# A decoder block with an expert layer: the V rows of token block 1 gathered a token per partition and summed on VectorE, where TensorE summed them before

## The chip, the cores and the metric
One Trainium2 chip, one NeuronCore. The metric is the device time of one execution in microseconds (us), as the median of several. The kernel before has 2984.19 us (three runs, 2970.84 to 2986.44).

The engines are named as in the profile: PE is TensorE's matmuls and PEld its weight loads, DVE is VectorE, ACT ScalarE, POOL GpSimd and SP the sync engine, which here only issues DMAs.

## The reference, cut to what matters
One layer on 1024 tokens of width 1024, all float32: an input projection, an mLSTM and a differential attention over four heads each, an output projection, and then the part that the change touches, a retrieval of single-neuron experts for each token (`peer`):

```
s = einsum('thpk,hpnk->thpn', q, sub_keys)        # 8 heads, two halves of 128 keys
sv, si = top_k(s, 16); cand = sv0 + sv1; fv, fpos = top_k(cand, 16)
eidx = the 16 experts of each head; g = softmax(fv)      # 8 x 16 = 128 experts per token
act = gelu(einsum('td,thkd->thk', xb, u_tab[eidx]))
out = einsum('thk,thkd->td', g * act, v_tab[eidx])       # the sum over V rows
```

The two tables `u_tab` and `v_tab` have 16384 rows of 1024 numbers (4 KB a row). So a block of 128 tokens needs 128 x 128 rows of each: 128 gathers of 128 rows (512 KB each) of U, and as many of V.

## The kernel before, in words
**Blocks and groups.** The 1024 tokens are eight blocks of 128. They go through the front part (projections, mLSTM, attention, output projection, keys, top-k) in three groups: blocks 0 and 1, blocks 2 to 4, blocks 5 to 7 (`GROUPS`, L36).

**Two ways for the experts.** Blocks 2 to 5 (`DENSE`, L37) gather nothing: in the last part of the kernel (`dense`, L1274) they are multiplied with all rows of the tables, 128 steps of 128 experts; a step has a score part (`s_mm`, L1330, matmul L1343), a gate part on VectorE (`s_gate`, L1346) and a value part (`v_step`, L1363, matmul L1375). Their gates are laid out as tables by `gates` (L1212): VectorE writes one-hot tiles `oh` (L1258 and L1259, two buffers), TensorE multiplies them (`ps_g`, L1243), ScalarE copies the result (L1245), and it goes to DRAM. Blocks 0, 1, 6 and 7 gather.

**A gathered block.** `g_u` (L1018) gathers, for expert number k of each token, a U row per partition, and VectorE multiplies it with the token's row and sums over it (L1028). When all 128 are done, `g_w` (L1033) makes the weights w = g * gelu(z). Then come 128 gathers of V rows (`g_v`, L1070), in one of two forms:
- the blocks in `ROWSUM` (L39; 6 and 7) gather as for U, one row per token, with the index tile `ei`, and VectorE adds each tile, times one column of w, to a sum in PSUM (`g_v_rows`, L1054, L1062 and L1064). `finish_rows` (L1154) ends the block.
- the others (0 and 1) transpose w and the indices on TensorE (L1044 to L1051), so that gather t brings the 128 experts of token t, one per partition. Each gather is used in four matmuls (a 128x32 weight, which is a column of w in a strip of zeros, `strips`, L994, and 256 columns, L1090), which the trace counts as eight: 1024 for a block. Two gathers are used together, so they come in bursts of 16. VectorE copies two columns of weights into a strip now and then (L1088). `finish` (L1171) ends the block.

**Buffers.** All gathered tiles, U and V, share six buffers (`GB`, L997, tag `gx`). A gather waits, on POOL's queue, for the buffer that the use of an earlier one gives back. The sum `ga` is one PSUM tile for all blocks (L1040).

**Order of the work.** The gathers are one generator (`gathers`, L1104) that runs behind the other work: each step of a projection calls `tick` (L306), which advances it by `RG` = 1.6 gathers (L70); the use of a gather is written `LAG` = 4 gathers later (L1110). V goes before U, two by two. When the front part has been written, what is left of it is written with `later(PU)` (L1500), and the dense part with `later(PD)` (L1507). A planner (a list scheduler with its own estimate of durations) then fixes one order for each engine and queue: of the work that it believes ready, the one written earliest goes first; `later` moves work back in this ranking, `PU` = 100000 places and `PD` = 300000; the gates of block 5, written in the dense part, are taken forward again by `LP` = 310000 (L1430). So the ranks are: front, gates of block 5, left-over gathers, dense. On the chip each engine runs its order strictly, and waits in it.

The part around the change, V of block 1, stands beside these pieces of the third group: the output projection (`front_out`, L803, two calls of `proj_R`, matmul L423), the query projection and the scores (`front_keys`, L859, four calls of `proj_T`, matmul L403, and L879), top-16 on VectorE (`key_tops`, L895), the routing of blocks 5, 6 and 7 (`route`, L937), the gate tables of blocks 3 to 5, and the first 14 score parts of the dense steps (`AHEAD`).

```
def g_v_rows(o, k):                                    # L1054
    vt = gat.tile([P, D], F32, tag="gx", name="gvr", bufs=GB)
    nc.gpsimd.indirect_dma_start(out=vt, out_offset=None, in_=pv,
                                 in_offset=bass.IndirectOffsetOnAxis(ap=o.ei[:, k:k + 1], axis=0))
    ...
            nc.vector.scalar_tensor_tensor(o.acc, vt, o.w[:, k:k + 1], o.acc, op0=OP.mult, op1=OP.add)
...
                mm = nc.tensor.matmul(o.acc[c * 32:(c + 1) * 32, q * QW:(q + 1) * QW],      # L1090
                                      st[:, q, 31 + 32 * i - r:63 + 32 * i - r],
                                      vt[:, c * QW:(c + 1) * QW], start=r == 0 and q % 2 == 0, stop=r == 31 and q % 2 == 1)
```

Of the kernel before, what the change touches and what calls it, by code (L numbers as in the profile page):

```python
# [35 lines left out]
GROUPS = [2, 3, 3]  # L36
DENSE = [2, 3, 4, 5]  # L37
MIXED = []
ROWSUM = [6, 7]  # L39
GSC = 2.0 ** 14  # L40
PG = 100000
PU = 100000
# [9 lines left out]
def kernel(ctx: ExitStack, tc: tile.TileContext, x, c_col, ada_w, ada_b, ada_bc, n1c,  # L52
# [980 lines left out]
    def g_w(o):  # L1033
# [6 lines left out]
        o.acc = psg.tile([P, D], F32, tag="ga", name="ga")  # L1040
        if o.tb in ROWSUM:
            o.w = w
# [11 lines left out]
# [6 lines that stand above are left out]
        def use():  # L1060
            if k == 0:
                nc.vector.tensor_scalar(o.acc, vt, o.w[:, 0:1], None, op0=OP.mult)  # L1062
            else:
                nc.vector.scalar_tensor_tensor(o.acc, vt, o.w[:, k:k + 1], o.acc, op0=OP.mult, op1=OP.add)  # L1064
            if k == P - 1:
                finish_rows(o.tb, o.acc)
                summing.remove(o)
        return use

    def g_v(o, m):  # L1070
        if o.tb in ROWSUM:
            return g_v_rows(o, m)
        r, q = divmod(m, 4)
        t = q * 32 + r
        vt = gat.tile([P, D], F32, tag="gx", name="gv", bufs=GB)
        got = nc.gpsimd.indirect_dma_start(out=vt, out_offset=None, in_=pv,  # L1076
                                           in_offset=bass.IndirectOffsetOnAxis(ap=o.eT[:, t:t + 1], axis=0))
        o.held.append((r, q, vt))

        def use():  # L1080
            if m % VB != VB - 1:
                return
            first = True
            for r, q, vt in o.held[:VB]:
                st = strips[(r // SR) % 2]
                i = r % SR
                if i == 0 and q == 0:
                    nc.vector.tensor_copy(st[:, :, 31:31 + 32 * SR:32], o.wT[:, :, r:r + SR])  # L1088
                for c in range(4):
# [3 lines that stand above are left out]
                    if first:  # L1093
                        tc.add_manual_dep(mm.ins, got.ins.name, together, reason="a batch's tokens stand side by side")
                        first = False
            del o.held[:VB]
            if m == P - 1:
                finish(o.tb, o.acc)
                summing.remove(o)
        return use  # L1100
# [468 lines left out]
```

## Time and profile before
| what | value |
|---|---|
| median of three runs | 2984.19 us (2970.84 to 2986.44) |
| the profiled execution, its own time | 2968.57 us |
| its span in the trace | 2966.8 us |
| mean granted TensorE clock in it | 0.962 of 2.4 GHz |
| busy: PE, PEld, DVE, ACT, POOL | 2783.8, 2079.3, 2382.0, 972.9, 1275.8 us |
| HBM traffic | 302 GB/s over the span |

A profile row gives busy time and counts; "idle before" is the time in which an engine stood still in front of such an instruction, with what released it. Matmuls overlap in the pipe, so the busy time of a group is the union of its matmuls and not count times mean. In a table of stretches the numbers in brackets count instructions, PEclk is the granted TensorE clock as a share of 2.4 GHz, and "DMA share" the mean busy share of the 16 DMA engines. An entry of VectorE with an accumulator output counts as two instructions.

### The profile page before, as it was taken

How to read it: one execution, taken by the hardware profiler on the slowest of the kernel's cores; microseconds unless marked ns; L12 is line 12 of the kernel's file. 1: busy time of each engine (PE TensorE's matmuls, PEld its weight loads, DVE VectorE, ACT ScalarE, POOL GpSimd, SP SyncE). 2: the span in 40 equal slices, each digit the busy share in tenths (PEclk: the TensorE clock that was granted, in tenths of full speed). 3: DMA queues.
4: the chain of work that ended last, by engine and by line, in shares of the span. 5: the costliest groups of instructions: out<-in, count | busy, mean ns of one | idle time of the engine just before them, and what ended most of it. 6: DMA issues, size and time to landing. Idle time of an engine off the chain costs nothing.

```text
span 2966.8 us, 40093 instructions
## 1 busy us (share of the span) xinstructions
PE 2783.8 (94%) x13686; PEld 2079.3 (70%) x13686; DVE 2382.0 (80%) x5489; ACT 972.9 (33%) x1701; POOL 1275.8 (43%) x1083
## 2 busy tenths in 40 slices
PE   6899999689999988999998999999999999999998
PEld 5547757466555765765666887877887778777776
DVE  5634999955998687457988998888988889888896
ACT  1432344312235355232454332322332323322332
POOL 0000277654555453334644555544544445444430
PEclk9989999689999998999998999999999999999999
DMA  8845699999999888998888999999999999899982
GB/s 281 254 135 182 201 359 343 328 341 336 328 343 314 311 289 305 322 340 286 306 299 302 325 326 335 318 323 345 325 333 323 325 332 337 327 318 316 319 318 78
DMA packets 395809, 899.48 MB, mean 303 GB/s; under 512 B 34754, under 2 KB 183234, under 8 KB 391508
## 3 DMA queue, kind: packets, MB, share of 16 engines
q0 software_dynamic: 147456, 536.94, 50.4%
q1 hardware_dynamic: 248148, 359.98, 35.9%
q8 instruction: 108, 1.77, 0.2%
q14 instruction: 97, 0.79, 0.1%
HBM read 846.45 MB, written 50.35 MB: 302 GB/s over the span
## 4 chain that ended last, share of the span: by engine, by line
PE 45%; DVE 22%; DMA 17%; issue 11%; POOL 3%; ACT 2%; SPq 0%; DVEq 0%; POOLq 0%; ACTq 0%
PE ps_pj L403 9%; PE ps_pj L423 8%; DMA Gt<-G_d 8%; PE ps_dA L1375 7%; PE ps_dS L1343 7%; DVE gu L1028 5%; DVE ga L1064 3%; PE ps_g L1243 3%; PE ga L1090 3%; DMA gu<-in_peer_u_dram,ei 2%; POOL gvr L1057 2%; DMA wmod<-in_ada_w_dram 2%; DVE dvs L1369 2%; DMA gv<-in_peer_v_dram,eT 2%; DVE dacc L1382 2%
## 5 line engine op out<-in xcount | busy, mean ns | idle before, releaser
L1024 POOL DMA_INDIRECT gu<-in_peer_u_dram,ei x512 | 652.1, 1274 | 969.1 <-DVE sv L912 349.5
L1375 PE MATMUL ps_dA<-dvs,W 128*128 128x512 f32 x2976 | 720.1, 397 | 44.4 <-DVE dvs L1369 21.1
L1343 PE MATMUL ps_dS<-dhT,us 128*128 128x512 f32 x3072 | 729.1, 391 | 1.2 <-POOL us L1336 1.2
L1375 PEld LDWEIGHTS ps_dA<-dvs,W 128*128 128x128 f32 x2976 | 566.8, 191 | 175.2 <-DVE dvs L1369 24.7
L1028 DVE SCALAR_TENSOR_TENSOR gu<-gu,h2r 128x1024 f32<-128x1024 f32 x512 | 619.8, 1220 | 73.2 <-DMA gu<-in_peer_u_dram,ei 65.8
L1343 PEld LDWEIGHTS ps_dS<-dhT,us 128*128 128x128 f32 x3072 | 575.5, 188 | 129.2 <-issue 7.4
L1057 POOL DMA_INDIRECT gvr<-in_peer_v_dram,ei x256 | 302.0, 1180 | 326.9 <-DVE ga L1064 191.7
L1076 POOL DMA_INDIRECT gv<-in_peer_v_dram,eT x256 | 273.3, 1068 | 269.7 <-PE ga L1090 151.6
L1064 DVE SCALAR_TENSOR_TENSOR ga<-gvr,w,ga 128x1024 f32<-128x1024 f32 x254 | 325.2, 1280 | 1.3
L1368 ACT ACTIVATE dvs<-dv 128x512 fp32r<-128x512 f32 x248 | 154.7, 626 | 321.6 <-PE ps_dA L1375 183.9
L403 PE MATMUL ps_pj<-hT,wr 128*128 128x384 f32 (+1 forms) x768 | 234.2, 460 | 2.8 <-ACT ae L598 2.8
L403 PE MATMUL ps_pj<-h2T,wr 128*128 128x384 f32 (+1 forms) x768 | 231.2, 454 | 0.0
L1344 ACT ACTIVATE ge<-ps_dS 128x512 f32<-128x512 f32 x128 | 76.3, 597 | 455.2 <-PE ps_dS L1343 455.2
L1245 ACT ACTIVATE stg<-ps_g 128x512 f32<-128x512 f32 x128 | 133.7, 1062 | 232.4 <-PE ps_g L1243 188.4
L403 PEld LDWEIGHTS ps_pj<-hT,wr 128*128 128x128 f32 x768 | 145.3, 194 | 79.4 <-issue 9.4
L403 PEld LDWEIGHTS ps_pj<-h2T,wr 128*128 128x128 f32 x768 | 142.2, 190 | 73.3 <-issue 9.9
L1258 DVE TENSOR_TENSOR oh<-iotah,dT 128x1024 f16<-128x1024 f16 x128 | 94.8, 746 | 118.1 <-PE ps_g L1243 115.2
L1352 DVE SCALAR_TENSOR_TENSOR ge<-ge,Gt 128x512 f32<-128x512 f32 x128 | 90.9, 719 | 121.8 <-DMA Gt<-G_d 120.1
L423 PE MATMUL ps_pj<-wr,hT 128*128 128x256 f32 (+1 forms) x672 | 181.8, 424 | 3.0 <-DMA wr<-in_w_in_dram 2.1
L1369 DVE TENSOR_TENSOR dvs<-dv,dvs 128x512 fp32r<-128x512 f32 x248 | 167.6, 682 | 9.7 <-ACT dvs L1368 9.7
L1090 PE MATMUL ga<-gv,strip 128*32 128x256 f32 x2048 | 147.8, 398 | 14.1 <-DMA gv<-in_peer_v_dram,eT 14.1
L423 PEld LDWEIGHTS ps_pj<-wr,hT 128*128 128x128 f32 x672 | 129.0, 197 | 44.1 <-issue 22.5
(294 smaller groups left out, 3311.6 us busy)
## 6 DMA issues: line engine op xcount, KB each, us to landing
u<-in_peer_uT_dram SPq DMA_DIRECT2D x128, 512.0 KB
dv<-in_peer_v_dram SPq DMA_DIRECT2D x248, 256.0 KB
wr<-in_w_in_dram SPq DMA_DIRECT2D x168, 256.0 KB
G_d<-stg SPq DMA_DIRECT2D x32, 1024.0 KB
Gt<-G_d SPq DMA_DIRECT2D x15, 2048.0 KB
wmod<-in_ada_w_dram SPq DMA_DIRECT2D x48, 512.0 KB
wr<-in_peer_w_query_dram SPq DMA_DIRECT2D x96, 256.0 KB
wr<-in_w_out_dram SPq DMA_DIRECT2D x48, 256.0 KB
```

What stands on the lines that cost most here:

```text
L403: nc.tensor.matmul(out[f], w2[:, kh, f * P:(f + 1) * P], hT[:, kb, :n], start=kb == 0 and f % k == 0, stop=kb == NC - 1 and f % k == k - 1)
L423: nc.tensor.matmul(out[f], hT[:, kb, f * P:(f + 1) * P], wk[:, kh], start=kb == 0 and f % k == 0, stop=kb == NC - 1 and (f % k == k - 1 or ...
L1024: nc.gpsimd.indirect_dma_start(out=u, out_offset=None, in_=pu, in_offset=bass.IndirectOffsetOnAxis(ap=o.ei[:, k:k + 1], axis=0))
L1028: nc.vector.scalar_tensor_tensor(u, u, 1.0, o.h2, op0=OP.mult, op1=OP.mult, accum_out=o.z[:, k:k + 1])
L1057: nc.gpsimd.indirect_dma_start(out=vt, out_offset=None, in_=pv, in_offset=bass.IndirectOffsetOnAxis(ap=o.ei[:, k:k + 1], axis=0))
L1064: nc.vector.scalar_tensor_tensor(o.acc, vt, o.w[:, k:k + 1], o.acc, op0=OP.mult, op1=OP.add)
L1076: got = nc.gpsimd.indirect_dma_start(out=vt, out_offset=None, in_=pv, in_offset=bass.IndirectOffsetOnAxis(ap=o.eT[:, t:t + 1], axis=0))
L1090: mm = nc.tensor.matmul(o.acc[c * 32:(c + 1) * 32, q * QW:(q + 1) * QW], st[:, q, 31 + 32 * i - r:63 + 32 * i - r], vt[:, c * QW:(c + 1) * ...
L1343: nc.tensor.matmul(ps, us[:, a, c], hT[:, b, c, sl], start=c == 0 and i == 0, stop=c == NC - 1 and i == 2)
L1368: nc.scalar.activation(vs[:, 0], v, AF.Copy)
L1369: nc.vector.tensor_sub(vs[:, 1], v, vs[:, 0])
L1375: nc.tensor.matmul(pacc[tb], w[:, a, tb * P:(tb + 1) * P], vs[:, b], start=jj == 0 and i == 0, stop=jj == J - 1 and i == 2)
```

## The change
Block 1 joins the blocks whose V rows are gathered a token per partition and added on VectorE. Block 0 alone keeps the matmul form. Nothing else is edited; `g_w`, `g_v` and the planner's order follow from the list.

```diff
 GROUPS = [2, 3, 3]
 DENSE = [2, 3, 4, 5]
 MIXED = []
-ROWSUM = [6, 7]
+ROWSUM = [1, 6, 7]
 GSC = 2.0 ** 14
```

## Rows read from the trace of the kernel before
**Rows 1.** The page's head: span, then busy time of each engine.
```profile
span 2966.8 us, 40093 instructions
...
PE 2783.8 (94%) x13686; PEld 2079.3 (70%) x13686; DVE 2382.0 (80%) x5489; ACT 972.9 (33%) x1701; POOL 1275.8 (43%) x1083
```
**Rows 2.** Stretches: length, busy PE, PEld, DVE, ACT, POOL, then PEclk, DMA share, GB/s.
```profile
1190.00:1300.00 110.00, 106.83 (x725) 76.26 (x724) 40.76 (x97) 30.90 (x51) 40.31 (x40) 0.98 0.96 348
1300.00:1412.00 112.00, 110.47 (x732) 67.25 (x731) 83.33 (x445) 30.46 (x42) 47.76 (x45) 1.00 0.84 295
1412.00:1490.00 78.00, 72.28 (x501) 48.40 (x502) 76.41 (x283) 37.26 (x38) 47.91 (x36) 0.98 0.84 297
1490.00:1594.00 104.00, 93.72 (x649) 71.02 (x642) 86.00 (x132) 59.41 (x74) 50.27 (x35) 0.94 0.84 296
1594.00:2890.00 1296.00, 1262.70 (x5470) 1035.89 (x5470) 1161.38 (x1592) 386.84 (x583) 623.92 (x504) 0.99 0.93 327
2890.00:2967.00 77.00, 66.75 (x288) 53.20 (x286) 52.28 (x88) 18.16 (x41) 0.00 (x0) 0.97 0.23 79
```
**Rows 3.** The same stretches, tile `gv` alone: PE, PEld, POOL (block 1's V).
```profile
1190.00:1300.00 110.00, 20.09 (x274) 7.64 (x274) 40.31 (x40) 0.98 0.96 348
1300.00:1412.00 112.00, 22.68 (x334) 9.16 (x334) 43.05 (x43) 1.00 0.84 295
1412.00:1490.00 78.00, 18.04 (x237) 6.85 (x240) 30.60 (x29) 0.98 0.84 297
1490.00:1594.00 104.00, 13.71 (x186) 5.00 (x179) 19.80 (x18) 0.94 0.84 296
```
**Rows 4.** Groups by line: whole span (three rows), then VectorE from 1190 to 1412.
```profile
L1028 DVE SCALAR_TENSOR_TENSOR gu<-gu,h2r 128x1024 f32<-128x1024 f32 x512 | 619.8, 1220 | 73.2 <-DMA gu<-in_peer_u_dram,ei 65.8
L1064 DVE SCALAR_TENSOR_TENSOR ga<-gvr,w,ga 128x1024 f32<-128x1024 f32 x254 | 325.2, 1280 | 1.3
L1090 PE MATMUL ga<-gv,strip 128*32 128x256 f32 x2048 | 147.8, 398 | 14.1 <-DMA gv<-in_peer_v_dram,eT 14.1
...
L1088 DVE COPY strip<-wT 128x8 f32<-128x8 f32 x11 | 2.1, 200 | 9.0 <-PE ga L1090 9.0
```
**Rows 5.** Who waited for whom, 1190 to 1412: us in total, times, longest.
```profile
POOL gv L1076 <- PE ga L1090: 116.8, 34, 14.2
...
DVE oh L1258 <- PE ps_g L1243: 74.8, 19, 8.5
POOL gv L1076 <- DVE eT L1049: 26.8, 1, 26.8
```
**Rows 6.** The chain that ended last, 1337 to 1353: start us, us, what.
```profile
1337.07 6.45 PE ps_pj L403 x20
1343.52 1.00 PE ga L1090 x16
...
1351.18 1.49 PE ps_pj L403 x4
```
**Rows 7.** Groups by line: VectorE from 1412 to 1594, POOL from 1190 to 1594.
```profile
L1028 DVE SCALAR_TENSOR_TENSOR gu<-gu,h2r 128x1024 f32<-128x1024 f32 x4 | 7.1, 1766 | 0.0
...
L1336 POOL TENSOR_TENSOR us<-u,us 128x1024 fp32r<-128x1024 f32 x18 | 44.1, 2452 | 24.4 <-ACT us L1335 24.2
```
**Rows 8.** Stretches, columns as in rows 2: U of block 0 and 1; mid of dense.
```profile
400.00:500.00 100.00, 95.79 (x384) 64.87 (x384) 95.69 (x226) 43.59 (x100) 74.63 (x52) 0.93 0.96 338
500.00:600.00 100.00, 67.36 (x295) 47.44 (x293) 87.65 (x220) 36.45 (x101) 61.26 (x51) 0.73 0.92 327
...
2200.00:2300.00 100.00, 97.77 (x425) 80.41 (x424) 90.49 (x124) 29.16 (x45) 49.86 (x43) 0.98 0.94 331
```
**Rows 9.** Tile `gu` in a stretch: DVE, POOL; then VectorE's last V sum and `finish_rows`.
```profile
1700.00:1800.00 100.00, 44.96 (x76) 52.00 (x40) 1.00 0.96 336
...
2879.76 1.28 DVE L1064 SCALAR_TENSOR_TENSOR ga<-gvr,w,ga 128x1024 f32<-128x1024 f32 x1
...
2893.71 1.28 DVE L1168 SCALAR_TENSOR_TENSOR fx<-fx,gms 128x1024 f32<-128x1024 f32 x1
```

## The prediction
> **What bounds the kernel now.** I read the page's head first: TensorE is busy 94% of the span and VectorE 80% [rows 1], so the tempting reading is that work taken from TensorE is time gained. That is an average over stages. So next the stretches around block 1's V sums [rows 2], and in the same stretches the V tile alone [rows 3]. The tile's 128 gathers (40, 43, 29, then 18 less a few of neighbours at the cuts) run from 1190 us into the last of these four stretches: this is where the change acts. Four stages lie there. A, 1190 to 1300, the output projection: TensorE 106.8 of 110 us, VectorE only 40.8, DMA 0.96. B, 1300 to 1412, query projection and top-16: TensorE 110.5 of 112, VectorE 83.3. C, 1412 to 1490, the routing: VectorE 76.4 of 78, which is its limit. D, 1490 to 1594, block 5's gates ahead of the dense part: VectorE 86.0 and TensorE 93.7 of 104. After that the dense part: TensorE 1262.7 of 1296, VectorE 1161.4 (90%) [rows 2].
>
> Then the waits tell what VectorE's free time is [rows 5]. In A and B it stands 74.8 us before a one-hot tile until TensorE has read the older one: it waits because it is early, not because it has nothing to do, so this time is real room. POOL waits 116.8 us for TensorE to give gather buffers back, so the gathers are paced by their users and not by DMA. The dense part can't begin before routing and gates, and 14 score parts ahead are all that TensorE may do meanwhile; so the path to the dense part runs over TensorE in A and B and over VectorE from C on.
>
> **What the change removes.** (1) 1024 matmuls on TensorE, 74.5 us by the four stretches (20.1, 22.7, 18.0, 13.7) [rows 3], half of the 147.8 us of both blocks [rows 4]. (2) The disturbance of each burst: 20 projection matmuls in a row take 6.45 us, 0.32 each, but four behind a burst take 1.49 instead of 1.29 [rows 6]: 0.2 us for each of 64 bursts, 13 us. So TensorE loses some 87 us, of which A and B hold (20.1 + 22.7) x 87 / 74.5 = 50. (3) Sixteen strip copies of 0.2 us [rows 4], 3 us of VectorE, and the index transposes, for which POOL stood 26.8 us before the first V gather [rows 5]; the new gathers use the index tile that U used. (4) The block's end is four passes of 1024 columns on VectorE in either form; I count zero, and what hides a difference is that nothing waits for this block's output; without that cover it would be an operation or two, under 3 us.
>
> **What it adds.** 128 sums on VectorE at 1280 ns [rows 4], 164 us. The gathers stay 128 of the same 512 KB, on POOL and DMA alike, so both are costed at nothing.
>
> What could make a sum dearer is POOL's subtraction of 2452 ns (18 of them in C and D): beside it the U product takes 1766 ns instead of 1220 [rows 7, 4]. The bounds are 1.28 and 1.28 x 1766 / 1220 = 1.85 us for the sums that fall there, up to 51, so 0 to 29 us more; I take 1.28, since the row of the operation itself is nearest. The Trainium skill, SBUF — State Buffer, section Who interferes with whom, says that only a VectorE instruction with two inputs in SBUF contends with a GpSimd instruction that reads it. The sum has its second input in PSUM, so by that page the price is the lower bound, and no row before shows a sum beside a subtraction.
>
> **Where the 128 sums come to stand.** The projections of A and B have 16 and 32 ticks at 1.6 gathers, so 77 gathers are ranked among this front work; the other 51 rank behind the front and block 5's gates, but ahead of the dense part.
>
> *A to C.* VectorE has 200.5 us of work in these 300 us [rows 2]. The 77 sums add 98.6, the copies take off 3: 296 of 300. TensorE's 50 us would let the stage end earlier only if VectorE could follow, and it can't: it has become the limit here. The question is how densely it runs. The best long stretch of this trace in which it carries gathers is 95.7% (400 to 500), the next 87.7%, and there TensorE fell to 67.4 us and the granted clock to 0.73 of 2.4 GHz [rows 8]. At 100% the stage ends at 1486, at 95.7% 296 takes 309 (+9), at 87.7% 337 (+37). Because sums hold their place in a strict order and may stand before a gather that has not landed, with top-16 behind them and the routing and TensorE's 14 score parts behind that, I take 94%: 315, **+15**, and keep -4 and +37. Gathers that start without the transpose give back some 5: **+10**.
>
> *D.* 51 sums are 65 us; VectorE has 18 free of 104 [rows 2], so some 15 go in and the rest moves into the dense part. TensorE is 13.7 us lighter here, but a sum between two one-hot writes holds up the pair behind it, and behind that ScalarE's copies and the first gate. Ends: -14 (TensorE set the pace) and +19 (each of the 15 on the path); **+8**, nearer to the second, since VectorE is 98% busy just before.
>
> *Dense.* 35 or so sums are left: 45 us of VectorE against 135 us free in 1296 [rows 2]. Gathers go at 40 per 100 us [rows 9], so the end of V moves from 2880 by 35 x 2.5 = 88 us, to about 2970, plus the shift of the start, while the last dense product ends the span at 2967 plus that same shift. Both finish nearly together. Beside gathers TensorE loses 2.2 us of 100 [rows 8], 2 us over those 88; with the 14 us from the last V sum to the end of its block [rows 9] sticking out in part: **+5**, ends 0 and +30.
>
> **The sum.** 10 + 8 + 5 = 23 us: 2968.6 becomes about 2992 for the profiled execution. That execution lies 15.6 us under the median of the runs, so against the median 2984.2 + 23 = **3007 us**, 0.8% slower. Half a per cent, 15 us, is about what a measurement of this kernel can tell from no change.
>
> **A page that weighs against the gain on TensorE.** In stage B the matmul row says 110.5 of 112 us, but the weight loads only 67.3 [rows 2]. The Trainium skill, Perfetto Trace Analysis, section Identifying the Most-Contended Engine, holds matmul busy time a poor measure of how near TensorE is to its limit, and weight loads a better one. By it TensorE has room in B and its relief is worth less than 50 us even where VectorE can follow; by the bursts of rows 6 it was worth 1.2 us each. I let it weigh on the chance of the first rival only.
>
> **Rivals.** *TensorE's relief counts (faster).* The planner ranks the sums but places them only when it believes their gather landed and VectorE free; were 30 of the 77 to slip behind the routing, A to C would hold 296 - 38 = 258 us of VectorE, 274 at 94%, 26 us less than now; D gains up to its 14; the slipped sums cost some 5 in dense. 2984 - 35 = 2949. For it: 74.8 us of waiting for TensorE is room by the trace, and TensorE's waits for V gathers, 14.1 us over both blocks [rows 4], halve. Against it: that the matmuls of this block did run in A and B, 608 of 1024 [rows 3], so the planner did place gathers there. It decides from about 20 slipped sums. Chance 0.20.
>
> *Even.* VectorE runs A to C at 98 to 100% and D's relief pays for the rest: -5 to +10, 2986. The 98% of stage C [rows 2] speaks for it, the gap between 95.7 and 87.7% in rows 8 against. Chance 0.26.
>
> *The gathers end the kernel (much slower).* If D takes no sums and 10 of the 77 slip too, 61 x 2.5 = 152 us: V ends at 2880 + 152 + 10 = 3042, its block 14 us later at 3056, 89 over the span. Some of it comes back, because behind 2890 VectorE is only 52.3 of 77 us busy [rows 2] and the sums could follow each other at 1.3 us instead of 2.5: about half. 2984 + 55 = 3039. It decides from some 40 sums left at the start of dense. Chance 0.12.
>
> My forecast has the other 0.42. That the change does nothing is excluded by the list itself.
>
> **How the numbers follow.** Slower by over 0.5% (above 2999): 0.42 + 0.12 = 0.54; within, 0.26; faster, 0.20. The low end 2952 takes in most of the first rival; the high end adds the upper bounds of A to C and D to the forecast's start, 37 + 19 = 56 less 5, with some of the dense bound: 3055. The forecast's own range is 2999 to 3030.
>
> **What the profile after would show.** VectorE above 90% from 1190 to the dense part, the wait for `ps_g` before one-hot tiles shrunk from 74.8 to under 25 us, TensorE below 90% in B or C, its clock dipping where it stands. The routing would end near 1500 and the first value matmul come some 18 us later than before. V sums of block 1 would still run beyond that point, some 35 of them, and the last V sum of block 7 would lie near 2980. I am wrong if the dense part begins earlier than before, if under 10 sums of block 1 are left when it begins, or if its 1296 us grow by over 30.

## The result, and the profile after

The changed kernel takes 3089.44 us (median of six, 3083.22 to 3093.86); the kernel before, on the same chip, 2976.14 us (six, 2970.84 to 2986.44). The ratio is 1.038 with an interval of 1.0362 to 1.0397: 113 us slower. The forecast was 3007 us with a range up to 3055. Its direction held; its size was a fifth of what came, and the range missed.

First the page's head, two lines of its 40 slices (77.3 us each), and three groups (busy, mean ns of one, idle time before them and what ended it); they answer to [rows 1], [rows 4] and the `ps_g` wait of [rows 5].

```profile
span 3090.4 us, 38119 instructions
...
PE 2714.1 (88%) x12658; PEld 2058.3 (67%) x12658; DVE 2512.9 (81%) x5589; ACT 968.9 (31%) x1697; POOL 1294.4 (42%) x1083
...
PE   6899999689999988899221799999999999999998
...
PEclk9989999699999988999655799999999999999999
...
L1064 DVE SCALAR_TENSOR_TENSOR ga<-gvr,w,ga 128x1024 f32<-128x1024 f32 x381 | 489.3, 1284 | 7.3 <-DMA gvr<-in_peer_v_dram,ei 5.6
L1243 PE MATMUL ps_g<-oh 128*128 128x128 f16 x1024 | 139.6, 296 | 144.0 <-DVE oh L1259 131.6
```

TensorE lost 1028 instructions and 69.7 us of busy time, and VectorE gained 130.9 us; the forecast had 74.5 to 87 us and 161 us. But slices 20 to 22, 1468 to 1700 us, read 2, 2, 1: TensorE stands for nearly 200 us in front of the dense part. The share of busy time of a whole engine says nothing of that (VectorE went from 80 to 81%); the slices do.

Next, where the time went. The first value matmul marks the start of the dense part: 1587.9 us before, 1720.6 after (least, median and longest ns, then first and last start).

```profile
L1375 PE MATMUL ps_dA<-dvs,W x2976: 387/389/796, 1587.9 to 2934.8; 128*128 128x512 f32 x199
```

```profile
L1375 PE MATMUL ps_dA<-dvs,W x2976: 387/389/795, 1720.6 to 3058.4; 128*128 128x512 f32 x199
```

So the kernel is cut there (length, then busy time of PE, PEld, DVE, ACT, POOL, then PEclk, DMA share, GB/s); the first fence is the kernel before, the second the changed one.

```profile
1190.00:1588.00 398.00, 381.36 (x2593) 261.90 (x2591) 280.50 (x947) 153.99 (x197) 184.89 (x154) 0.99 0.88 311
1588.00:2967.00 1379.00, 1331.39 (x5760) 1090.13 (x5760) 1219.66 (x1687) 409.04 (x628) 625.28 (x505) 0.98 0.89 313
```

```profile
1190.00:1720.00 530.00, 314.48 (x1610) 245.21 (x1608) 491.69 (x1204) 151.99 (x198) 278.85 (x219) 0.76 0.86 302
...
1720.00:3090.00 1370.00, 1328.47 (x5760) 1089.05 (x5760) 1145.53 (x1550) 411.56 (x631) 544.11 (x437) 0.98 0.83 289
```

The dense part is 9 us shorter and the stretch ahead of it 132 us longer: the whole loss lies between 1190 us and the first value matmul. The 123.6 us between the two spans are 132 less 9 (the medians, 113 apart, come from more executions). In that stretch VectorE has 211 us more work and 79 us less idle time (117.5 before, 38.3 after): 211 - 79 = 132. Such a sum comes out for any engine; what marks VectorE as the limit is that it stands for only 38 of the 530 us, while TensorE, which stood for 17 us of 398 before, now stands for 216.

What the 211 us are is told by VectorE's groups from 1190 to 1715 us.

```profile
L1064 DVE SCALAR_TENSOR_TENSOR ga<-gvr,w,ga 128x1024 f32<-128x1024 f32 x127 | 162.3, 1278 | 4.5 <-DMA gvr<-in_peer_v_dram,ei 4.2
L1028 DVE SCALAR_TENSOR_TENSOR gu<-gu,h2r 128x1024 f32<-128x1024 f32 x69 | 83.6, 1224 | 15.2 <-DMA gu<-in_peer_u_dram,ei 14.9
```

All 128 sums are there (the first is L1062), 164 us. And 69 U products of block 6 are there, where the kernel before had 4 [rows 7]: another 76 us. These 240 us are less 29 us that the same stretch no longer holds or that became shorter (8 gates of the dense part, the strip copies, the folds of L971 and L972: 29.4 us before, 15.1 now). The products were not added by the change, and they did not come forward in time either. Here is their line from 1190 to 1800 us, before and after, and then the start of block 7's routing after:

```profile
L1028 DVE SCALAR_TENSOR_TENSOR gu<-gu,h2r x82: 1209/1214/3420, 1564.5 to 1789.1; 128x1024 f32<-128x1024 f32 x82
```

```profile
L1028 DVE SCALAR_TENSOR_TENSOR gu<-gu,h2r x100: 1178/1224/1293, 1561.8 to 1799.8; 128x1024 f32<-128x1024 f32 x100
```

```profile
1589.68 1.22 DVE L974 TENSOR_TENSOR ge<-pos,startc 128x2048 f16<-128x2048 f16 x1
```

Block 6's first product starts at 1564.5 us before and at 1561.8 after, behind block 1's V in both. What moved is the rest: before, all routing had ended at 1518.5 us and the first dense gate came at 1584.4; now block 7's routing had not begun, and the gate comes at 1719.2.

Stage by stage, answering to [rows 2]:

```profile
1190.00:1300.00 110.00, 96.64 (x497) 79.03 (x496) 90.87 (x150) 31.99 (x55) 46.10 (x42) 0.91 0.93 348
1300.00:1400.00 100.00, 95.57 (x423) 66.75 (x422) 99.21 (x358) 34.47 (x46) 38.85 (x34) 0.98 0.84 291
1400.00:1480.00 80.00, 79.41 (x395) 64.68 (x393) 78.44 (x220) 33.52 (x39) 58.20 (x40) 1.00 0.86 303
1480.00:1520.00 40.00, 8.03 (x41) 6.04 (x40) 40.00 (x95) 6.12 (x6) 26.21 (x20) 0.64 0.85 272
1520.00:1560.00 40.00, 0.47 (x1) 0.18 (x1) 39.31 (x103) 4.13 (x3) 14.38 (x14) 0.50 0.58 186
...
1640.00:1680.00 40.00, 1.11 (x8) 0.83 (x8) 31.65 (x58) 0.20 (x1) 32.98 (x24) 0.50 0.91 313
1680.00:1720.00 40.00, 16.80 (x128) 13.98 (x128) 37.58 (x64) 19.82 (x26) 15.78 (x15) 0.50 0.95 352
1720.00:1760.00 40.00, 35.05 (x137) 28.17 (x138) 38.10 (x63) 14.47 (x22) 18.53 (x15) 0.84 0.93 322
```

From 1300 to 1560 us VectorE runs at 98 to 100%. TensorE keeps up until about 1490 us, because gate tables and its score parts are there to fill it (by then 16 of them, 384 matmuls of L1343, where the prediction had 14 as the most); then it has nothing that is ready. Two tables of waits say for what: first from 1190 to 1480 us, then from 1480 to 1715 us (who waited for whom: us in total, times, longest). The row of VectorE in the second is all that VectorE itself waited for there.

```profile
DVE oh L1258 <- PE ps_g L1243: 10.4, 7, 5.1
```

```profile
PE ps_g L1243 <- DVE oh L1259: 120.0, 18, 58.9
...
PEld ps_gt L1235 <- DVE ii L972: 39.4, 2, 24.8
...
PE ps_gt L1235 <- DVE gs L1222: 32.0, 1, 32.0
...
DVE gu L1028 <- DMA gu<-in_peer_u_dram,ei: 14.9, 14, 2.3
...
SPq L1366 <- DVE ef L1014: 70.4, 1, 70.4
```

The 74.8 us for which VectorE stood before one-hot tiles [rows 5] have become 10.4; in return TensorE waits 120 us for one-hot tiles, 39 us for the routing's `ii` and 32 us for the gates' `gs`, all from VectorE, and behind 1480 us VectorE does not wait for TensorE at all. SP's queue (the last row, from the same view of that queue) stands for one long wait too, 70.4 us; whether that costs anything is asked below.

Why VectorE comes late with them, although routing ranks ahead of left-over gathers: VectorE's instructions around 1502 us, in block 5's routing, and around 1607 us, in block 7's, in order of time (start us, us). The routing of a block ends with its second `ii` (L972).

```profile
1501.29 0.28 DVE L971 TENSOR_TENSOR pr<-pr 128x256 f16<-128x256 f16 x1
...
1501.77 1.26 DVE L1064 SCALAR_TENSOR_TENSOR ga<-gvr,w,ga 128x1024 f32<-128x1024 f32 x1
1502.95 0.28 DVE L972 TENSOR_TENSOR ii<-pr 128x128 f32<-128x128 f16 x1
...
1503.41 1.27 DVE L1064 SCALAR_TENSOR_TENSOR ga<-gvr,w,ga 128x1024 f32<-128x1024 f32 x1
1504.60 1.21 DVE L978 TENSOR_TENSOR pr<-ge,rown 128x2048 f16<-128x2048 f16 x1
...
1505.94 1.26 DVE L1064 SCALAR_TENSOR_TENSOR ga<-gvr,w,ga 128x1024 f32<-128x1024 f32 x1
1507.12 0.68 DVE L971 TENSOR_TENSOR pr<-pr 128x1024 f16<-128x1024 f16 x1
...
1508.00 1.26 DVE L1064 SCALAR_TENSOR_TENSOR ga<-gvr,w,ga 128x1024 f32<-128x1024 f32 x1
1509.17 0.41 DVE L971 TENSOR_TENSOR pr<-pr 128x512 f16<-128x512 f16 x1
```

```profile
1602.87 0.68 DVE L971 TENSOR_TENSOR pr<-pr 128x1024 f16<-128x1024 f16 x1
1603.47 1.21 DVE L1028 SCALAR_TENSOR_TENSOR gu<-gu,h2r 128x1024 f32<-128x1024 f32 x1
...
1604.62 1.21 DVE L1028 SCALAR_TENSOR_TENSOR gu<-gu,h2r 128x1024 f32<-128x1024 f32 x1
...
1608.98 1.23 DVE L1028 SCALAR_TENSOR_TENSOR gu<-gu,h2r 128x1024 f32<-128x1024 f32 x1 [1.94 <-DMA gu<-in_peer_u_dram,ei]
...
1610.74 0.42 DVE L971 TENSOR_TENSOR pr<-pr 128x512 f16<-128x512 f16 x1
1611.07 1.22 DVE L1028 SCALAR_TENSOR_TENSOR gu<-gu,h2r 128x1024 f32<-128x1024 f32 x1
```

The routing is a chain: each fold (L971) needs the one before it. Between two steps of the chain stands one sum of 1.28 us in the first stretch (with short steps of other blocks' top-16), and U products and one-hot writes in the second, where two folds of 0.68 and 0.42 us start 7.9 us apart; one of the products there waits 1.94 us for its gather, with the chain behind it. The lower rank did not keep the sums out. The likely reason is that where the planner has put down a step of the chain it does not yet take the next for ready, while a sum is; its estimates stand in no trace, so this is read from the order that came out. Of the 128 sums 100 were done when block 5's routing began (1487 us); the other 28 came during the routing of blocks 5 and 6. Of the 70 products ahead of the first dense gate (before: 4), 42 stand within block 7's routing. In the kernel before its joints held 18 one-hot writes, which the gates need anyway, and it took 27.0 us; now it takes 78.7. The last `ii` of the routing shows the price (min, median and longest ns, first and last start, before and then after): its start went from 1518.5 to 1668.4 us.

```profile
L972 DVE TENSOR_TENSOR ii<-pr x6: 264/292/3121, 1441.0 to 1518.5; 128x128 f32<-128x128 f16 x6
```

```profile
L972 DVE TENSOR_TENSOR ii<-pr x6: 276/284/291, 1502.9 to 1668.4; 128x128 f32<-128x128 f16 x6
```

### The profile page after: what moved, and what is told of

Its sections match the earlier page's. It is cut to its first block, busy times and chain, and to the rows that moved or that the text cites. A ratio compares the mean times of both kernels' runs of the same rounds, so it can differ in the third digit from the quotient of the medians.

```text
span 3090.4 us, 38119 instructions
## 1 busy us (share of the span) xinstructions
PE 2714.1 (88%) x12658; PEld 2058.3 (67%) x12658; DVE 2512.9 (81%) x5589; ACT 968.9 (31%) x1697; POOL 1294.4 (42%) x1083
## 5 line engine op out<-in xcount | busy, mean ns | idle before, releaser
L1024 POOL DMA_INDIRECT gu<-in_peer_u_dram,ei x512 | 660.3, 1290 | 953.4 <-DVE sv L912 363.9
L1375 PE MATMUL ps_dA<-dvs,W 128*128 128x512 f32 x2976 | 715.9, 395 | 37.4 <-DVE dvs L1369 16.2
L1343 PE MATMUL ps_dS<-dhT,us 128*128 128x512 f32 x3072 | 724.5, 391 | 1.4 <-POOL us L1336 1.4
L1375 PEld LDWEIGHTS ps_dA<-dvs,W 128*128 128x128 f32 x2976 | 565.7, 191 | 166.9 <-DVE dvs L1369 20.9
L1343 PEld LDWEIGHTS ps_dS<-dhT,us 128*128 128x128 f32 x3072 | 577.9, 189 | 121.8 <-POOL us L1336 2.0
L1057 POOL DMA_INDIRECT gvr<-in_peer_v_dram,ei x384 | 449.3, 1170 | 493.8 <-DVE ga L1064 245.3
L1064 DVE SCALAR_TENSOR_TENSOR ga<-gvr,w,ga 128x1024 f32<-128x1024 f32 x381 | 489.3, 1284 | 7.3 <-DMA gvr<-in_peer_v_dram,ei 5.6
L1243 PE MATMUL ps_g<-oh 128*128 128x128 f16 x1024 | 139.6, 296 | 144.0 <-DVE oh L1259 131.6
L1243 PEld LDWEIGHTS <-oh 128*128 128x128 f16 x1024 | 112.7, 120 | 170.6 <-DVE oh L1259 139.5
L1076 POOL DMA_INDIRECT gv<-in_peer_v_dram,eT x128 | 136.7, 1068 | 74.8 <-issue 24.1
L1382 DVE TENSOR_TENSOR dacc<-dacc,ps_dA 128x512 f32<-128x512 f32 x240 | 155.8, 684 | 6.5 <-PE ps_dA L1375 6.5
```

What stands on the lines that cost most here:

```text
L1024: nc.gpsimd.indirect_dma_start(out=u, out_offset=None, in_=pu, in_offset=bass.IndirectOffsetOnAxis(ap=o.ei[:, k:k + 1], axis=0))
L1243: nc.tensor.matmul(pg[:, r * P:(r + 1) * P], oh[:, 0, :, r], oh[:, 2 + i, :, r], start=i == 0, stop=i == np_ - 1)
L1343: nc.tensor.matmul(ps, us[:, a, c], hT[:, b, c, sl], start=c == 0 and i == 0, stop=c == NC - 1 and i == 2)
L1375: nc.tensor.matmul(pacc[tb], w[:, a, tb * P:(tb + 1) * P], vs[:, b], start=jj == 0 and i == 0, stop=jj == J - 1 and i == 2)
L1382: nc.vector.tensor_add(o, o, pacc[tb])
```

## The experiments

The theory: the first dense gate can't come before VectorE's sums and products that the order puts ahead of it, so the start of the dense part moves by their number times their length. Rivals: SP's queue, blocked for 70 us, delays the tables; the low clock does it; TensorE's relief was worth something and hides part of a larger loss; the dense part would have no room for these sums either. For each run the table has the sums and products that its planned order puts ahead of the first dense gate, VectorE's time for them (1.28 us and 1.3 us each, the reading of the accumulator included; shortened sums at their measured length), the first value matmul, and the length from there to the end of the span; the last two are of one profiled execution each. Ratios are to the kernel before in the same session.

| kernel | sums, products ahead | us of VectorE | dense starts | length | median | ratio (95%) |
|---|---|---|---|---|---|---|
| before | 0, 4 | 5 | 1587.9 | 1379 | 2976.14 | 1 |
| the change | 128, 70 | 255 | 1720.6 | 1370 | 3089.44 | 1.038 (1.0362 to 1.0397) |
| sums_behind_routing | 115, 0 | 147 | 1613.2 | 1400 | 3007.21 | 1.0097 (1.0063 to 1.013) |
| sum_of_4_columns | 128, 4 | 28 | 1576.2 | 1380 | 2956.26 | 0.9944 (0.9925 to 0.9964) |
| sum_of_512_columns | 128, 21 | 117 | 1624.6 | 1376 | 2999.98 | 1.0077 (1.0055 to 1.0099) |
| tables_on_act_queue | 128, 70 | 255 | 1708.0 | 1370 | 3096.28 | 1.0413 (1.0374 to 1.0452) |
| u_behind_routing | 128, 18 | 187 | 1652.1 | 1384 | 3030.42 | 1.0168 (1.0151 to 1.0185) |
| sums_behind_tables | 101, 0 | 129 | 1586.9 | 1387 | 2982.85 | 1.0035 (1.0012 to 1.0058) |
| few_sums_in_front | 43, 0 | 55 | 1547.9 | 1478 | 3029.57 | 1.0172 (1.0155 to 1.0189) |
| 82_sums_in_front | 82, 0 | 105 | 1575.2 | 1427 | 3012.47 | 1.0129 (1.0108 to 1.015) |
| 72_sums_in_front | 72, 0 | 92 | 1553.5 | 1435 | 2999.52 | 1.0092 (1.0072 to 1.0112) |
| block_0_instead | 128, 50 | 229 | 1762.6 | 1364 | 3126.4 | 1.0494 (1.0476 to 1.0511) |
| before_with_hold | 0, 0 | 0 | 1573.6 | 1414 | 3002.58 | 1.0092 (1.0076 to 1.0108) |

**1. The left-over gathers behind the last routing (sums_behind_routing).** The last VectorE instruction of the routing is kept by name, and what is left over of the gathers may not be ordered ahead of it; the kernel has the helper for this, `after` (L295).

```diff
             decode(b, h0, nh)
+            routed[:] = [next(i.name for i in reversed(nc.cur_bb.bb.instructions) if i.engine == ET.DVE)]
...
-    with later(PU):
+    with later(PU), after(routed[0]):
         drain(streams[0])
```

> The kernel after, with one edge more: VectorE's share of the left-over gathers (sums of block 1 and U products of block 6 that were not written with the front's ticks) may not stand ahead of block 7's routing. The work is the same. Theory (VectorE's order: everything that VectorE does ahead of the first dense gate delays the dense part, and in the kernel after that is 128 sums and 70 U products where before there were 4 products): in the planned order 115 sums and no U product are left ahead of that gate, so VectorE has 286.5 - 13 + 147 = 420 us there, at the 93% of the kernel after 452 us: the dense part begins near 1640 instead of 1715 us and the time is 3015 us (2995 to 3035). Rival (it is the load as such: 164 us of sums have to be done somewhere and come back later): no change, 3075 to 3095. Rival (TensorE's low clock while it stands is the cost): the standing gets shorter too, so the same direction, but with a clock still at 0.5 the gain is under 40 us: above 3050.

3007.21 us, ratio 1.0097, within. Only 13 sums went behind the first dense gate, but with them all U products, and the dense part starts 107.4 us earlier:

```profile
L1375 PE MATMUL ps_dA<-dvs,W x379: 387/389/796, 1613.2 to 1799.9; 128*128 128x512 f32 x190
```

The count says 13 x 1.28 + 70 x 1.3 = 108 us. So the order makes most of the loss: 82 of the 113 us can be had back without touching the change itself.

**2. A sum of 4 columns (sum_of_4_columns).** Block 1's sums take in 4 of 1024 columns (the other 1020 keep the first of their 128 terms); gathers, DMAs and the number of instructions stay.

```diff
-                nc.vector.scalar_tensor_tensor(o.acc, vt, o.w[:, k:k + 1], o.acc, op0=OP.mult, op1=OP.add)
+                n = 4 if o.tb == 1 else D
+                nc.vector.scalar_tensor_tensor(o.acc[:, :n], vt[:, :n], o.w[:, k:k + 1], o.acc[:, :n], op0=OP.mult, op1=OP.add)
```

> The kernel after, but the sums of block 1 take in 4 of the 1024 columns (the others keep their first term), so each costs VectorE about 0.15 us instead of 1.28; gathers, buffers and TensorE's relief stay. VectorE has then 286.5 - 13 + 128 x 0.2 = 300 us ahead of the dense part, less than TensorE. Theory (VectorE's work is the whole price): the loss vanishes, and TensorE's relief of 75 to 87 us shows in part: 2900 to 2955 us. Rival (the row-a-token gathers themselves, their buffers or POOL cost something): above 2990. Rival (TensorE's relief is worth nothing, as its weight loads leave room): 2965 to 2985.

2956.26 us, ratio 0.9944: just above the expected range. All sums of the kernel in one row (the first numbers are the least, the median and the longest ns), then the start of the dense part; the added line moves L1064 to L1065 and L1375 to L1376:

```profile
L1065 DVE SCALAR_TENSOR_TENSOR ga<-gvr,w,ga x381: 175/1278/1291, 1196.7 to 2862.3; 128x1024 f32<-128x1024 f32 x127, 128x4 f32<-128x4 f32 x64
...
L1376 PE MATMUL ps_dA<-dvs,W x487: 387/389/796, 1576.2 to 1799.9; 128*128 128x512 f32 x163
```

With a sum of 175 ns the kernel is 133 us faster than the change and 19 us faster than before. The gathers and their DMAs, which this run keeps whole, cost nothing that shows. What is gone is the length of the sums together with 66 products: with shorter sums the routing ends at 1486.0 us, before the products start at 1558.8, so this run does not tell the two apart; run 5 does. It also bounds the gain: TensorE is free of the prediction's 87 us, VectorE still has 22 us of short sums, and 19 us come out at the end. Even if all 22 us lay on the path, no more than about 41 of the 87 would count in this order.

**3. A sum of 512 columns (sum_of_512_columns).** The same edit with 512 for 4.

```diff
+                n = 512 if o.tb == 1 else D
```

> As the run with 4 columns, with 512 of the 1024 columns (0.69 us a sum). In the planned order 128 sums and 21 U products stand ahead of the first dense gate: 286.5 - 13 + 88 + 27 = 389 us, at 93% 418: dense begins near 1608, time 2985 us (2965 to 3010) by the theory of VectorE's load and order. If the count of inserted instructions matters and not their length: within 30 us of the kernel after, above 3060.

2999.98 us, within; a sum takes 704 ns. Between a sum of 175, 704 and 1280 ns lie 44 and 89 us of median. With the second step 49 more products stand ahead as well (21, then 70): the length does not act only by itself.

**4. The late tables on another queue (tables_on_act_queue).** The table write of the late gates goes to ScalarE's queue, past SP's.

```diff
-                nc.sync.dma_start(G_d[db * (P // TS) + tg], stg)
+                (nc.scalar if mem.first is not None else nc.sync).dma_start(G_d[db * (P // TS) + tg], stg)
```

> The kernel after, but block 5's gate tables are written to memory by ScalarE's DMA queue instead of SP's. In the trace of the kernel after the table writes stood on SP behind a load of dense V rows that waited 70 us for block 7's routing to end, and TensorE and ScalarE stood 59 us. Theory (VectorE's order decides; the last 17 one-hot pairs come behind block 7's routing on VectorE anyway): under 15 us gained, 3075 to 3095 us. Rival (the blocked SP queue is what holds the gates, and the planner's order follows it): 30 to 60 us gained, 3030 to 3060.

3096.28 us, 1 us above the expected range, ratio 1.0413, an interval that overlaps the change's own: no gain (its profiled execution, at 3078.2 us of span, is the fastest of its five, so its start in the table is early too). SP's queue still stands for 68.0 us, but the tables no longer stand behind it, and nothing came of that. What waits there now, the loads of value rows (L1366, here L1367), was not moved.

**5. Only the products behind the routing (u_behind_routing).** All 128 sums stay where they are; block 6's U products may not come before block 7's routing has ended (`held` takes the name kept as in run 1).

```diff
-            nc.vector.scalar_tensor_tensor(u, u, 1.0, o.h2, op0=OP.mult, op1=OP.mult, accum_out=o.z[:, k:k + 1])
+            with after(held[0] if held and o.tb == 6 else None):
+                nc.vector.scalar_tensor_tensor(u, u, 1.0, o.h2, op0=OP.mult, op1=OP.mult, accum_out=o.z[:, k:k + 1])
```

> The kernel after, but only the U products of block 6 may not stand ahead of block 7's routing on VectorE; the sums of block 1 stay where they were, all 128 ahead of the routing's end. In the planned order 18 U products are left ahead of the first dense gate instead of 70. Theory (each instruction that VectorE does ahead of that gate costs its length): 52 x 1.3 us = 68 us less, 3089 - 68 = 3021 us (3005 to 3040). Rival (the sums alone are the price and the U products only fill time that is free anyway): 3075 to 3095.

3030.42 us, within. The start (L1377 is L1375 here):

```profile
L1377 PE MATMUL ps_dA<-dvs,W x312: 387/389/796, 1652.1 to 1796.9; 128*128 128x512 f32 x156
```

It is 68.5 us earlier; 52 products fewer at 1.3 us are 68. So the 113 us have two parts, and the prediction saw neither place: about 59 come back with these 52 products, and the other 54 stay with the sums and the 18 products that are left.

**6. The left-over gathers behind the late tables (sums_behind_tables).** The hold of run 1, moved behind block 5's gate tables in the dense part's code.

```diff
+            made = next(i.name for i in reversed(nc.cur_bb.bb.instructions) if i.engine == ET.DVE)
+            with later(PU - PD), after(made):
+                drain(streams[0])
...
-    with later(PU):
-        drain(streams[0])
```

> The kernel after, but all left-over gathers' work on VectorE, sums and U products, stands behind block 5's gate tables. Planned ahead of the first dense gate: 101 sums and no U product (115 and none in the run that held them behind the routing, 3007 us). Theory: 14 x 1.28 = 18 us off the start of the dense part, a few of them given back there, as more gathers have to end in it: 2990 to 3005 us. Rival (the dense part gives all of it back): 3003 to 3012.

2982.85 us, ratio 1.0035: better than expected, and the best kernel with the whole change in it, yet not faster than before. Its start, then one stretch (columns as above):

```profile
L1375 PE MATMUL ps_dA<-dvs,W x456: 388/389/795, 1586.9 to 1795.7; 128*128 128x512 f32 x152
...
1480.00:1580.00 100.00, 38.75 (x272) 31.07 (x270) 98.03 (x293) 44.12 (x48) 8.23 (x5) 0.54 0.37 129
```

Of the gathers that the front did not take none comes ahead of the gates any more, and 101 sums still do: so the front itself takes about a hundred, and not 77, and only 27 sums were left over. With them the dense part starts where it did before (1587.9). In the 100 us ahead of it TensorE is busy for 38.75 us at a granted clock of 0.54, near its level of 1.2 GHz, and the start is not late. In the change, too, VectorE waited for TensorE nowhere from 1480 to 1715 us, and from the last one-hot write to the first gate 5.8 us pass, 7.1 before. So the low clock goes with TensorE's standing still, and no part of the price here shows up as its own.

**7. Few sums in front (few_sums_in_front).** Run 6, and the rate of the gathers goes from 1.6 to 0.4 a tick before the third group's output projection.

```diff
+        if k == 2:
+            for w in background:
+                if streams and w[0] is streams[0]:
+                    w[1] = 0.4
         front_out(o)
```

> As the run with all left-over work behind the gate tables, and the gathers advance 0.4 per step instead of 1.6 from the third group's output projection on, so that only 43 sums are planned ahead of the first dense gate and 85 of them in the dense part. Theory (the dense part has no room: it already grew by 27 us in the run that held the sums behind the routing, and gathers go at one in 2.4 us): dense begins near 1575 us, 85 + 512 gathers take 1430 us, and the last block ends the kernel: 3000 to 3030 us. Rival (the forecast's own term: 35 sums left over cost the dense part 5 us, since VectorE has 10% free there): 2965 to 2985.

3029.57 us, within. The dense part starts at 1547.9, the earliest of all, and lasts 1478 us. The sums that it was left with end the kernel: the last matmul of the values starts at 2916 us, and the last four V sums of block 7 stand here:

```profile
L1064 DVE SCALAR_TENSOR_TENSOR ga<-gvr,w,ga x4: 1290/1290/1290, 3010.0 to 3014.4; 128x1024 f32<-128x1024 f32 x4
```

That is the mechanism of the prediction's third rival, reached on purpose: with 85 sums left over the dense part is 99 us longer than before.

**8, 9. The rates between (82_sums_in_front, 72_sums_in_front).** Run 7 with a rate of 1.2 and of 1.0.

```diff
-                    w[1] = 0.4
+                    w[1] = 1.2
```

> As the run with all left-over work behind the gate tables, with the gathers at 1.2 per step from the third group's output projection on: 82 sums planned ahead of the first dense gate. Between the runs with 101 (dense begins at 1587, last V sum at 2936) and 43 (1548 and 3014), by straight lines: dense begins near 1574, which alone would give a span of 2961, and the last V sum comes near 2962, its block some 10 us later, 2972. Theory (two ends that run against each other, the dense start by sums in front, the last gather by sums left over): 2965 to 2985 us, level with the kernel before and within 10 us of 101 sums. Rival (fewer sums in front always pay until the last block really ends the kernel): 2950 to 2962.

> The same at 1.0 gathers per step, 72 sums ahead of the first dense gate: dense begins near 1567, the last V sum near 2975, the block's end near 2986. Theory: 2980 to 3000 us, above the run with 82. Rival as there: below 2960.

3012.47 us, above what was expected, and 2999.52 us, within. Neither number between 43 and 101 sums is better than run 6, and fewer sums ahead even gave the better of these two. The starts follow the count (1575.2 and 1553.5), the dense lengths do not fall on a line. In both, as in run 7, the gathers end the kernel: the last V sum starts at 2989.9 and 2976.9 us, behind the last matmul of the dense part (2969.4 and 2943.4). In runs 6 to 9 a gather took 2.46 to 2.54 us from the start of the dense part to that sum, so each sum left over moves this end by as much. Each rate gives another planned order, and with it differences of 15 to 30 us that these runs do not explain.

**10. Block 0 in place of block 1 (block_0_instead).** If it is the place in the order that costs, another block should cost otherwise.

```diff
-ROWSUM = [1, 6, 7]
+ROWSUM = [0, 6, 7]
```

> Block 0 in place of block 1 on VectorE; block 1 keeps its matmuls. The same 128 sums lie in an earlier stage (610 to 1190 us of the kernel before, VectorE 43 to 95% busy), and the planned order has 50 U products ahead of the first dense gate instead of 70. Theory (VectorE's whole work ahead of the dense part counts, wherever it is put in, less what idle time it finds): 164 us of sums and 46 x 1.3 = 60 of U products, less the 117 us that VectorE had free from 1190 on and some of its free time before: 3030 to 3080 us. Rival (only the last stretch, from the third group's output projection on, is short of VectorE): 2960 to 2995 us.

3126.4 us, ratio 1.0494: worse than the change, and above the expected range. One stretch of it:

```profile
900.00:1000.00 100.00, 14.18 (x99) 11.07 (x99) 89.20 (x157) 20.60 (x19) 57.59 (x48) 0.50 0.79 266
```

TensorE was busy for 99.83 of the same 100 us before. Block 0's sums come beside the second group's front part, whose top-16 and routing are VectorE's too: that stage now stands as the third did in the change, and everything behind it comes later. I had counted on the later stages to make good more of it.

**11. The kernel before, with the hold (before_with_hold).** Run 6's edit on the kernel before.

> The control: the kernel before, block 1 on TensorE, with the same hold (the left-over gathers' VectorE work behind block 5's gate tables). Only 4 U products stood ahead of the first dense gate there, so VectorE has 5 us less to do. Theory: within 0.4% of the kernel before, 2966 to 2990 us. Rival (the hold itself is worth something, whatever the place of the sums): more than 15 us faster, which would make the 2983 us of the held kernel after a poor result beside it.

3002.58 us, ratio 1.0092, where at most 2990 was expected. The hold brings the start 14 us forward and lengthens the dense part by 35, as all left-over gathers come later; 144 of block 1's 1024 matmuls now stand in the dense part too, where there were none. So in this kernel the hold has a price of its own, and beside a kernel with the same hold the change is faster: a ratio of 1.0035 (1.0012 to 1.0058) against 1.0092 (1.0076 to 1.0108), 0.57% or 17 us. Which part of the long dense parts of runs 7 to 9 is this price, and which is the sums, was not taken apart.

What follows from all: where block 1's sums stay in the third group's stretch, the start moves by about what VectorE must do ahead of the gates. Against the change, 108, 68, 126, 150 and 163 us less work (runs 1, 5, 6, 8, 9) brought it 107.4, 68.5, 133.7, 145.4 and 167.1 us forward. Each start is of one execution, and run 4, with the change's own counts, starts 12.6 us earlier; agreement closer than that is luck. With little work ahead the rule ends: with 0 to 55 us the starts lie between 1548 and 1588 in no order (the kernel before, runs 2, 7 and 11). Run 3 lies apart: 138 us less work, 96 us earlier; why was not tried.

## Why the prediction was wrong

**Right.** VectorE becomes the limit from 1300 us on (98 to 100% busy up to 1600 us; in stage A, where over 90% was forecast, it is busy for 90.9 of 110 us) and TensorE stands behind it, at a falling clock; the wait of 74.8 us shrinks to under 25 (10.4); gathers and DMAs cost nothing (run 2); the first value matmul comes later; the first rival, that TensorE's relief makes the kernel faster, falls. Direction and sign of each term ahead of the dense part held.

**Right: the price of a sum.** It was taken as 1.28 us between 1.28 and 1.85. Over all 381 sums of the changed kernel, those beside POOL's 18 subtractions of 1341 to 1494 us among them, the row is (least, median, longest ns):

```profile
L1064 DVE SCALAR_TENSOR_TENSOR ga<-gvr,w,ga x381: 1232/1285/1304, 1198.3 to 2833.5; 128x1024 f32<-128x1024 f32 x191
```

Not one is longer than 1304 ns; the 16 that ran beside a subtraction took 1264 to 1291. The lower bound holds, and the trace agrees with the Trainium skill, SBUF — State Buffer, section Who interferes with whom: a VectorE instruction with at most one input in SBUF does not contend with GpSimd. (The page says so outside VectorE's two-port modes; the prediction's "only" leaves that out.) The upper bound was misread: 1766 ns is the mean of four U products [rows 7], of which one took 3420 and the others 1211 to 1216. The long one started at 1564.48 us in the kernel before, beside this subtraction:

```profile
1564.31 2.51 POOL L1336 TENSOR_TENSOR us<-u,us 128x1024 fp32r<-128x1024 f32 x1 [4.06 <-ACT us L1335]
```

So the product lost 2.2 us there, which the bound of 1.85 us for an instruction understates. The folds that became shorter were of this kind: six of them stood beside a subtraction before and took 2.3 to 3.2 us each.

**The step that failed: "Where the 128 sums come to stand", stage D.** The prediction had 77 sums in the front, "some 15" in D, and "the rest moves into the dense part", since left-over gathers rank behind front and gates. All 128 stood ahead of the first dense gate, 100 of them ahead of the routing, and 70 products of block 6 with them; the falsifier named, under 10 sums left, came true with none left. The mistake was to read a rank as a barrier. Rank decides between two instructions that the planner takes for ready at once; between the dependent short steps of a chain (routing at 0.28 to 1.21 us a step) lower-ranked ones of 1.2 to 1.3 us came in (28 sums and 51 products up to the last `ii`), and run 1, which forbids this by a dependency, brings the start 107.4 us forward. I had named the danger ("a sum between two one-hot writes holds up the pair behind it") and priced it for 15 sums instead of the 28 sums and 66 products that came.

**The term left out.** No line of the sum spoke of block 6's products. They follow block 1's V, and start at about 1562 us as before (1564.5); but by then the sums had pushed block 7's routing back behind them, and they fill its joints. Run 5 prices 52 of them at about 59 us, half the loss.

**The numbers of the front.** 48 ticks of 1.6 gave 77; with the rest held back (run 6), 101 stand ahead. The rates of runs 6 to 9 tell why: 101, 43, 82 and 72 sums at 1.6, 0.4, 1.2 and 1.0 a tick are 24 sums and 48 for each gather a tick. So the 48 ticks were right, and 24 sums more that do not hang on them were overlooked. In A to C the estimate was +10. Run 6 has 99 of its sums ahead of the routing and starts at 1586.9, run 11, the kernel before with the same hold, at 1573.6: +13. The size came out right in part by luck: the routing itself ends at 1558.2 (below) where run 11 has 1516.3, later than the upper bound of +37, and the stage behind it made good most of that.

```profile
L972 DVE TENSOR_TENSOR ii<-pr x6: 269/291/294, 1494.8 to 1558.2; 128x128 f32<-128x128 f16 x6
```

The loss is made by what came between the routing's steps and ahead of the late gates.

**The dense term.** +5 for 35 sums was not tested by the changed kernel, where none were left. With the rest held back the dense part is longer than before's by 21 us with 13 sums left (run 1), 8 with 27 (run 6), 48, 56 and 99 with 46, 56 and 85 (runs 8, 9 and 7). The last three lie past the 40 sums from which the prediction let the gathers end the kernel, and there they did; for fewer the single executions give no rule. What part is the hold's own price stays open: run 11 has 35 us, but with 144 matmuls of block 1 in its dense part, which the other runs do not have.

**The page on the most contended engine.** The Trainium skill, Perfetto Trace Analysis, section Identifying the Most-Contended Engine, holds matmul busy time a poor measure of how near TensorE is to its limit, from which the prediction took that the relief is worth less than its length. Run 2 agrees: of the prediction's 87 us between 19 and 41 reached the end; it does not tell whether TensorE's own room or VectorE's order is the reason. The rival that it weighed on fell.

## What to carry to other kernels

Work moved to an engine that also carries a long chain of short dependent steps can land in the joints of that chain in spite of a lower rank, unless a dependency keeps it out; count what the planner will find ready there. And a chain that slips back meets the work that used to come behind it, so count that too, not only what is added. When such a loss is suspected, hold the moved work behind the chain's last step and see whether the start of the next stage moves by count times length. Look at slices rather than shares: nearly 200 us of standing TensorE went with a change of VectorE's share of the span by a single point.

## What the runs showed of the hardware that was not expected

The granted TensorE clock read 0.50, the level of 1.2 GHz, in each of the stretches of 40 us from 1520 to 1720 us, in which TensorE was busy for 0.47 to 16.8 us; in the next 40 us, with 35.05 us of work, it is 0.84 and over the rest 0.98. What it did meanwhile was short and waited for VectorE, which never waited for it there, so that this lower clock cost nothing that the start of the dense part shows (run 6). I had also not expected how little 87 us less of matmuls is worth here on an engine that is busy 94% of the span (run 2: 19 us, with VectorE's sums shortened), nor that a subtraction on POOL holds up a product with both inputs in SBUF by 2.2 us and a sum with one input in PSUM not at all.
